# Last 256 features of the last embedding by token, with PSUM banks of their own; query, key and value weight pieces at other places in their tiles

## The chip, the cores and the metric

The kernel runs on one core of one Trainium2 chip. The metric is device microseconds of one execution; the median of several runs counts. A profile is one execution taken by the hardware profiler: TensorE (PE, its weight loads as PEld), VectorE (DVE), ScalarE (ACT), GpSimd (POOL) and the queue that issues DMAs (SP).

## The reference

Two layers over 256 tokens of 1024 features, in float32:

```python
for i in range(DEPTH):                                   # 2 layers
    h = x + 0.5 * swiglu(rms_norm(x, norm_ffn1[i]), w_ffn1_in[i], w_ffn1_out[i])
    u = rms_norm(h, norm_mix[i])
    q, k, v, c, g = jnp.split(u @ w_in[i], splits, axis=-1)
    q = rms_norm(q by head, q_norm[i]); k = rms_norm(k by head, k_norm[i])
    y_attn = window_attention(q, k, v, sink[i], rel_bias) @ w_attn_out[i]
    c_val, c_gate = jnp.split(c, 2, axis=-1)
    c = depthwise_conv(c_val * jax.nn.sigmoid(c_gate), conv_w[i], conv_b[i])   # 31 taps
    y_conv = jax.nn.silu(layer_norm(c, ...)) @ w_conv_out[i]
    g_attn, g_conv = jnp.split(jax.nn.sigmoid(g), 2, axis=-1)
    h = h + (g_attn * y_attn + g_conv * y_conv) @ w_o[i]
    h = h + 0.5 * swiglu(rms_norm(h, norm_ffn2[i]), w_ffn2_in[i], w_ffn2_out[i])
    x = h + (p[i] @ w_pe_proj[i]) * jax.nn.sigmoid(rms_norm(h, norm_pe[i]) @ w_pe_gate[i])
```

The last line is the embedding that the change touches in layer 2; queries, keys and values come out of `u @ w_in`.

## The kernel before, in words

Activations lie by feature: 128 features on the partitions, 256 tokens along the row, eight such blocks for the 1024 features (`x32`). A product of float32 accuracy is made of three matmuls: weights and activations are each split into a high and a low part, and high x high, high x low and low x high are added up in PSUM (`mm3`, whose matmuls have line 339). As a rule a 128x128 block of weights is loaded into PE and 256 columns of activations move past it. One such product of 1024 features takes 8 blocks x 3 = 24 matmuls. In a profile's row `out<-moving,loaded` the first name behind the arrow is what moves.

`Weights` streams all weights through `raw` tiles by DMA and prepares pieces ahead of their use: ACT writes the high part (`w_hi`, line 108), DVE the low part (`w_lo`, line 109), each into one of 7 tiles of 128x1024 words, 4096 bytes a partition. Where a piece starts in SBUF follows from the tile. Before the change each piece starts at its tile's start, a multiple of 256 bytes. Tiles of activations that move past weights are 2112 words for eight blocks (`rows`, with 64 spare words) and start at word 4 of their tile; with the sizes of all tiles ahead of them that is 48 bytes past a multiple of 64 for all of them, high and low parts 256 bytes apart within 512.

In the mixer keys and values (lines 733 to 735) and queries (777 to 779) are made by token: there the activations of 128 tokens are loaded, and the piece of weights moves, 256 columns for keys and values and 512 for queries. Each makes 48 matmuls in a layer. Behind them ACT, POOL and DVE make head norms (`junk`, `ms`, `rh`, lines 709 to 719). DVE runs the 31 taps of the depthwise convolution for four blocks (`y`, line 669) beside all this; at the mixer's end it normalizes `y` by token (`six`, `mv`, `rs`, `yn`, lines 971 to 978), and PE transposes `yn` back (`ps_yc`, line 991). ACT turns gates by a sigmoid (line 932) in between, and DVE multiplies by them (line 956).

The embedding of a layer (`embed`): `project(i)` makes p @ w_pe_proj for four blocks of features into a PSUM tile `pe[i]`; `one(f)` makes the gate of block f (24 matmuls into `ps_pe`), and its evacuation scales by the norm (DVE, line 1117), takes the sigmoid (ACT, line 1118), multiplies by the projection (DVE, line 1120) and adds to `x32` (DVE, line 1121). In layer 2 `put(f)` then transposes the block to tokens (PE, `ps_out`, line 1132), copies it to an output tile `ot` (ACT, line 1134) that shares two buffers with the product `hh`, and issues a DMA (SP, line 1135).

PSUM tiles of one bank come from a pool of four (`mm_tile`), those of two banks from a pool of two (`at_tile`). The order of instructions on each engine is set by a scheduler when the program is built, except where the code pins it. An evacuation is queued and issued behind the first product of the next group.

Of the kernel before, what the change touches and what calls it, by code (L numbers as in the profile page):

```python
# [15 lines left out]
P = 128  # L16
T = 256
# [15 lines left out]
NEG = -1e9  # L33
LOOK = 6
RAW_BUFS = 5
DMA_SCRATCH = 8192
BACKGROUND = 800
WEIGHTS_LAG = 100
ATTN = 7
# [7 lines left out]
class Weights:  # L47
# [14 lines left out]
        self.units.append((k, n, sources))  # L62
        return len(self.units) - 1

    def spec(self, k, n, pieces):

        self.specs.append((k, n, pieces, False))

    def raw_spec(self, unit, k, c0, n):
        self.specs.append((k, n, [(unit, 0, c0, 0, n)], True))  # L70

    def limit(self):
        held = [p[0] for s in self.specs[self.next_get : self.next_prep] if s[3] for p in s[2]]
# [12 lines left out]
    def prep_upto(self, i):  # L86
        nc = self.nc
        while self.next_prep <= min(i, len(self.specs) - 1):
            k, n, pieces, as_is = self.specs[self.next_prep]
            for u, *_ in pieces:  # L90
                self.load_upto(u + RAW_BUFS - 2)
                if u >= self.next_load:
                    return
            if as_is:
                ((u, k0, s0, _, w),) = pieces
                self.ready[self.next_prep] = self.raw[u][:, k0 : k0 + k, s0 : s0 + w]
                self.next_prep += 1
                continue
            hi = self.w_pool.tile([P, KD * P], F32R, name="w_hi")
            lo = self.w_pool.tile([P, KD * P], F32R, name="w_lo")  # L100
            hv = hi[:, : k * n].rearrange("p (k n) -> p k n", n=n)
            lv = lo[:, : k * n].rearrange("p (k n) -> p k n", n=n)
            step = k // self.parts
            for a, (u, k0, s0, d0, w) in ((a, p) for a in range(0, k, step) for p in pieces):
                at = slice(a, a + step)
                src = self.raw[u][:, k0 + a : k0 + a + step, s0 : s0 + w]
                parts = (
                    nc.scalar.copy(out=hv[:, at, d0 : d0 + w], in_=src),  # L108
                    nc.vector.tensor_tensor(  # L109
                        out=lv[:, at, d0 : d0 + w],  # L110
                        in0=src,
                        in1=hv[:, at, d0 : d0 + w].bitcast(F32),
                        op=ALU.subtract,
                    ),
                )
                if self.pin:
                    for ins in parts:
                        self.pin(ins)
                    self.pin = None
            self.ready[self.next_prep] = (hv, lv)  # L120
            self.next_prep += 1
# [34 lines left out]
def encoder_kernel(ctx: ExitStack, tc: tile.TileContext, a: dict, out: bass.AP):  # L156
# [18 lines left out]
    def mm_tile(name):  # L175
        return mmp.tile([P, 512], F32, name=name, tag="mm")
# [84 lines left out]
    def mix_specs(l):  # L261
        w = a["w_in"][l]
        c0 = QD + 2 * P

        def conv_specs(j, n):
            uv = cols_unit(w, KD, c0 + j * P, n * P)
            ug = cols_unit(w, KD, c0 + CD + j * P, n * P)
            for c in range(n):
                ws.spec(KD, P, [(uv, 0, c * P, 0, P)])
                ws.spec(KD, P, [(ug, 0, c * P, 0, P)])  # L270

        conv_specs(0, 2)
        ukv = cols_unit(w, KD, QD, 256)
        for i in range(2):
            ws.spec(KC, 256, [(ukv, i * KC, 0, 0, 256)])
        for i in range(2):
            uq = cols_unit(w[i * KC * P : (i + 1) * KC * P], KC, 0, QD)
            for k in range(0, KC, 2):
                ws.spec(2, QD, [(uq, k, 0, 0, QD)])
        conv_specs(2, 2)  # L280
        g0 = QD + 2 * P + 2 * CD
        for j in range(8):
            u = cols_unit(w, KD, g0 + j * 256, 256)
            for c in range(2):
                ws.spec(KD, P, [(u, 0, c * P, 0, P)])
        w = a["w_attn_out"][l]
        for j in range(2):
            src = w[:, j * 512 : (j + 1) * 512].rearrange("(v c p) n -> v p c n", v=2, p=HD)
            u = ws.unit(KC, 512, [
                (lambda v: v[0:HD], src[0]),  # L290
                (lambda v: v[HD : 2 * HD], src[1]),
            ])
            for c in range(2):
                ws.raw_spec(u, KC, c * 256, 256)
        w = a["w_conv_out"][l]
        for j in range(2):
            u = cols_unit(w, KC, j * 512, 512)
            for c in range(2):
                ws.spec(KC, 256, [(u, 0, c * 256, 0, 256)])
        w = a["w_o"][l]  # L300
        for j in range(4):
            u = cols_unit(w, KD, j * 256, 256)
            for c in range(2):
                ws.spec(KD, P, [(u, 0, c * P, 0, P)])

    def pe_specs(l):
        up = cols_unit(a["w_pe_proj"][l], 2, 0, 1024)
        for c in range(2):
            ws.spec(2, 512, [(up, 0, c * 512, 0, 512)])
        for j in range(4):  # L310
            u = cols_unit(a["w_pe_gate"][l], KD, j * 256, 256)
            for c in range(2):
                ws.spec(KD, P, [(u, 0, c * P, 0, P)])

    for l in range(L):
        ffn_specs(a["w_ffn1_in"][l], a["w_ffn1_out"][l], quick=l == 0)
# [76 lines left out]
    def flush_urgent():  # L393

        with tc.high_priority(offset=300):
            flush()
# [705 lines left out]
    def embed(l, x_in, st, xn, stat):  # L1102
        pw = [ws.get(), ws.get()]
        pl = late["pT"]
        pe = [None, None]

        def project(i):
            pe[i] = at_tile("ps_pp").rearrange("p (f t) -> p f t", t=T)
            for f in range(4):
                mm3(pe[i][:, f, :], pw[i], pl, cols=slice(f * P, (f + 1) * P))  # L1110

        def one(f):
            ps = mm_tile("ps_pe")

            def evac():
# [5 lines left out]
                nc.vector.tensor_tensor(out=x32[:, f, :], in0=hh, in1=x32[:, f, :], op=ALU.add)  # L1121
                if xn is not None:
                    emit_x(f, pcol("norm_ffn1", l + 1, f), xn, stat)
                elif f < KD - 1:
                    ws.later(2, lambda: put(f))

            group([lambda: mm3(ps[:, :T], ws.get(), x_in)], evac)

        def put(f):
            po = mm_tile("ps_out")  # L1130
            for t in range(2):
                nc.tensor.transpose(po[:, t * P : (t + 1) * P], x32[:, f, t * P : (t + 1) * P], ident)
            ot = tmp.tile([P, 2, P], F32, name="ot", tag="hh")
            nc.scalar.copy(out=ot, in_=po[:, :T].rearrange("p (t q) -> p t q", t=2))
            nc.sync.dma_start(out[0].rearrange("(t p) d -> p t d", p=P)[:, :, f * P : (f + 1) * P], ot)

        project(0)
        for f in range(KD):
            if f == 3:
                project(1)  # L1140
            ws.rest = 1 if f == KD - 1 else 0
            one(f)
        flush_urgent()
        ws.rest, ws.pin = 0, tc.keep_in_program_order
        if xn is None:
            ws.finish()
            put(KD - 1)

    def embed_load(l):
        p_ld = tmp.tile([P, 2, PLE], F32, name="p_ld", tag="gu")  # L1150
# [16 lines left out]
    for l in range(L):  # L1167
# [8 lines left out]
        with tc.tile_pool(name="ffn2_pool", bufs=1) as hp:  # L1176
            xe = tuple(rows(hp, KD, "xe_" + part) for part in "hl")
            stat = Stat()
            ffn(hp, l, x_cur, st, "norm_pe", xe, stat, {0: lambda: embed_load(l), 4: lambda: embed_input(hp)})
            x_cur, st = xe, stat.finish(4)  # L1180
            xn, stat = (new_x("xa", f"xn{l}") if l + 1 < L else None), Stat()
            embed(l, x_cur, st, xn, stat)
            x_cur, st = xn, stat.finish(3)
# [39 lines left out]
```

## Time and profile before

| | |
|---|---|
| median of 3 runs | 1092.87 us (1092.22 to 1093.42) |
| profiled execution | 1092.97 us |
| its span, first to last instruction | 1091.2 us |
| granted TensorE clock | 0.998 of full speed |
| busy: PE, DVE, ACT, POOL | 99%, 75%, 57%, 8% |

The span is what the profile's rows add up to; the 1.77 us by which the execution is longer lie around it. Rows give the start in us from the span's start, the time in us, the engine, the line, and in brackets how long the engine stood idle before and what ended that. Matmuls overlap: a row's time of one matmul is longer than the step from one to the next, so steps are read from starts, or from pieces of the chain with their counts.

### The profile page before, as it was taken

What the parts mean: (1) busy time and instruction counts of PE and PEld (TensorE: products, weight loads), DVE (VectorE), ACT (ScalarE), POOL (GpSimd) and SP (SyncE); (2) the same over time, 40 slices, a digit from 0 to 9 for tenths busy, and PEclk for the clock granted to TensorE, in tenths of its full rate; (3) what the DMA queues carried; (4) which work ended last, traced back from release to release, by engine and by line L of the source; (5) the groups of instructions that cost most, each with busy time, mean ns of one, the idle gap of its engine ahead of it and who ended that gap; (6) DMA issues with size and microseconds to landing.
All of it is one profiled execution on the core that took longest, in us unless ns stands there. A gap on an engine that the chain in (4) does not pass through costs nothing.

```text
span 1091.2 us, 22048 instructions
## 1 busy us (share of the span) xinstructions
PE 1082.8 (99%) x9178; PEld 1061.2 (97%) x9178; DVE 822.0 (75%) x1229; ACT 621.0 (57%) x1040; POOL 84.5 (8%) x123
## 2 busy tenths in 40 slices
PE   9999999999999999999999999999999999999997
PEld 9999999999999999999999999999998999999997
DVE  6876666899989766666886666669999986666664
ACT  7655445676767555445765554557776665554552
POOL 2000001210002000001100000113100100000110
PEclk9999999999999999999999999999999999999999
DMA  9876556556066646546556564566634666564531
GB/s 310 281 250 220 179 166 226 177 170 178 15 230 231 220 166 219 182 167 232 185 177 216 171 210 148 186 229 195 154 117 139 212 200 216 172 207 148 188 115 39
DMA packets 195695, 203.01 MB, mean 186 GB/s; under 512 B 3731, under 2 KB 188899, under 8 KB 195596
## 3 DMA queue, kind: packets, MB, share of 16 engines
q1 hardware_dynamic: 195564, 201.60, 55.9%
q8 instruction: 72, 1.18, 0.4%
q14 instruction: 27, 0.22, 0.1%
q10 hardware_dynamic: 32, 0.01, 0.0%
HBM read 200.53 MB, written 1.06 MB: 185 GB/s over the span
## 4 chain that ended last, share of the span: by engine, by line
PE 92%; DVE 2%; ACT 2%; DMA 1%; issue 1%; POOL 0%; SPq 0%; DVEq 0%; ACTq 0%; POOLq 0%
PE ps_gu L339 41%; PE ps_fo L339 22%; PE ps_g L339 8%; PE ps_c L339 4%; PE ps_pe L339 4%; PE ps_wo L339 4%; PE ps_co L1049 2%; DMA raw<-in_w_ffn_in_dram 1%; DVE w_lo L109 1%; PE ps_pp L339 1%; PE ps_s L818 1%; ACT g L932 1%; PE ps_o L874 1%; PE ps_q L778 1%; PE ps_q L777 1%
## 5 line engine op out<-in xcount | busy, mean ns | idle before, releaser
L109 DVE TENSOR_TENSOR w_lo<-raw,w_hi 128x1024 fp32r<-128x1024 f32 (+2 forms) x377 | 450.9, 1202 | 199.3 <-ACT w_hi L108 199.3
L108 ACT CAST w_hi<-raw 128x1024 fp32r<-128x1024 f32 (+2 forms) x377 | 387.7, 1034 | 365.1 <-PE ps_gu L339 191.0
L339 PE MATMUL ps_fo<-h_hi,w_hi 128*128 128x256 f32 x704 | 193.0, 275 | 0.0
L339 PE MATMUL ps_fo<-h_lo,w_hi 128*128 128x256 f32 x704 | 193.0, 275 | 0.0
L339 PE MATMUL ps_fo<-h_hi,w_lo 128*128 128x256 f32 x704 | 193.0, 275 | 0.0
L339 PEld LDWEIGHTS ps_fo<-h_lo,w_hi 128*128 128x128 f32 x704 | 131.8, 188 | 0.0
L339 PEld LDWEIGHTS ps_fo<-h_hi,w_lo 128*128 128x128 f32 x704 | 131.8, 188 | 0.0
L339 PEld LDWEIGHTS ps_fo<-h_hi,w_hi 128*128 128x128 f32 x704 | 131.8, 188 | 0.0
L443 POOL TENSOR_TENSOR sq_acc<-sq_acc,sq 128x256 f32<-128x256 f32 x56 | 52.6, 939 | 829.2 <-ACT sq L442 828.8
L669 DVE SCALAR_TENSOR_TENSOR y<-cpad,cw,y 128x256 f32<-128x256 f32 x240 | 101.8, 487 | 0.1
L339 PE MATMUL ps_gu<-xf0l,w_hi 128*128 128x256 f32 x352 | 97.0, 276 | 0.0
L339 PE MATMUL ps_gu<-xf1l,w_hi 128*128 128x256 f32 x352 | 97.0, 276 | 0.0
L339 PE MATMUL ps_gu<-xn0h,w_hi 128*128 128x256 f32 x352 | 97.0, 276 | 0.0
L339 PE MATMUL ps_gu<-xf0h,w_hi 128*128 128x256 f32 x352 | 96.9, 275 | 0.0
L339 PE MATMUL ps_gu<-xf1h,w_hi 128*128 128x256 f32 x352 | 96.9, 275 | 0.0
L339 PE MATMUL ps_gu<-xf0h,w_lo 128*128 128x256 f32 x352 | 96.9, 275 | 0.0
L339 PE MATMUL ps_gu<-xf1h,w_lo 128*128 128x256 f32 x352 | 96.9, 275 | 0.0
L339 PE MATMUL ps_gu<-xn0h,w_lo 128*128 128x256 f32 x352 | 96.8, 275 | 0.0
L339 PE MATMUL ps_gu<-xn0l,w_hi 128*128 128x256 f32 x352 | 96.8, 275 | 0.0
L339 PE MATMUL ps_gu<-x0h,w_lo 128*128 128x256 f32 x336 | 92.8, 276 | 0.2 <-DVE w_lo L109 0.2
L339 PE MATMUL ps_gu<-x0h,w_hi 128*128 128x256 f32 x336 | 92.9, 276 | 0.0
L339 PE MATMUL ps_gu<-x0l,w_hi 128*128 128x256 f32 x336 | 92.5, 275 | 0.0
(243 smaller groups left out, 2690.4 us busy)
## 6 DMA issues: line engine op xcount, KB each, us to landing
raw<-in_w_ffn_in_dram SPq DMA_DIRECT2D x86, 1024.0 KB
raw<-in_w_in_dram SPq DMA_DIRECT2D x30, 1024.0 KB
raw<-in_w_ffn_out_dram SPq DMA_DIRECT2D x32, 896.0 KB
raw<-in_w_ffn_out_dram SPq DMA_DIRECT2D x16, 1024.0 KB
raw<-in_w_o_dram SPq DMA_DIRECT2D x8, 1024.0 KB
raw<-in_w_pe_gate_dram SPq DMA_DIRECT2D x8, 1024.0 KB
raw<-in_w_attn_out_dram SPq DMA_DIRECT2D x8, 512.0 KB
raw<-in_w_conv_out_dram SPq DMA_DIRECT2D x4, 1024.0 KB
```

The costliest lines, as they stand in the source:

```text
L108: nc.scalar.copy(out=hv[:, at, d0 : d0 + w], in_=src),
L109: nc.vector.tensor_tensor(out=lv[:, at, d0 : d0 + w], in0=src, in1=hv[:, at, d0 : d0 + w].bitcast(F32), op=ALU.subtract,),
L339: mm = nc.tensor.matmul(ps, wa[:, k0 + k, cols], xa[:, kx, :], start=a, stop=b)
L443: nc.gpsimd.tensor_tensor(out=self.acc, in0=self.acc, in1=sq, op=ALU.add)
L669: last_tap[0] = nc.vector.scalar_tensor_tensor(out=y[:, i, :], in0=src, scalar=w, in1=y[:, i, :], op0=ALU.mult, op1=ALU.add)
L777: nc.tensor.matmul(o_, u[0][:, kx, ts], wh[:, k, :], start=kx == 0, stop=False)
L778: nc.tensor.matmul(o_, u[0][:, kx, ts], wl[:, k, :], start=False, stop=False)
L818: mm = nc.tensor.matmul(ps[v][:, c, :], qT[v * HD : (v + 1) * HD, c, qb * P : (qb + 1) * P], kT[v * HD : (v + 1) * HD, :], start=True, sto ...
L874: mm = nc.tensor.matmul(ps[v * HD : (v + 1) * HD, :], vt[:, b, v * HD : (v + 1) * HD], pT[v][:, b, :], start=b == 0, stop=b == 1,)
L932: tc.keep_in_program_order(nc.scalar.activation(out=gs, in_=gs, func=AF.Sigmoid))
L1049: mm = nc.tensor.matmul(ps[:, c, :], wa[:, k, c * P : (c + 1) * P], ya[:, k, :], start=(i, k) == (0, 0), stop=(i, k) == (2, KC - 1),)
```

## The change

1. In layer 2 the embedding's blocks 6 and 7, the last 256 features, are made by token. Their gate weights come as two pieces of 512 features x 256 columns (`pe_specs`), and `last_two` runs 24 matmuls for each half of the tokens into a PSUM bank of its own, with the weights moving. The projection of these features goes by token as well (`project`). The block's old values are transposed to tokens ahead of the gate, into another bank (`xt`), and the sum of that bank and the product goes straight to an output tile and out by DMA. The norm by token (`r_tok`) is made with the last statistic. Block 5's transposes, copy and DMA stand behind the last matmul (`put(KD - 3, last=True)`).
2. Output tiles of `put` share buffers with `sq` instead of `hh`; those of `last_two` with `gu`.
3. Weight tiles grow by 64 words, 256 bytes; keys' and values' pieces start at word 12 of theirs and queries' at word 32, all others at word 0. The DMA scratch shrinks from 8192 to 4096 bytes. All tiles behind it move by multiples of 256 bytes.

```diff
-DMA_SCRATCH = 8192
+DMA_SCRATCH = 4096
...
-            hi = self.w_pool.tile([P, KD * P], F32R, name="w_hi")
-            lo = self.w_pool.tile([P, KD * P], F32R, name="w_lo")
-            hv = hi[:, : k * n].rearrange("p (k n) -> p k n", n=n)
-            lv = lo[:, : k * n].rearrange("p (k n) -> p k n", n=n)
+            hi = self.w_pool.tile([P, KD * P + ROW], F32R, name="w_hi")
+            lo = self.w_pool.tile([P, KD * P + ROW], F32R, name="w_lo")
+            hv = hi[:, place : place + k * n].rearrange("p (k n) -> p k n", n=n)
+            lv = lo[:, place : place + k * n].rearrange("p (k n) -> p k n", n=n)
...
-            ws.spec(KC, 256, [(ukv, i * KC, 0, 0, 256)])
+            ws.spec(KC, 256, [(ukv, i * KC, 0, 0, 256)], 12)
...
-                ws.spec(2, QD, [(uq, k, 0, 0, QD)])
+                ws.spec(2, QD, [(uq, k, 0, 0, QD)], 32)
...
-                ws.spec(KD, P, [(u, 0, c * P, 0, P)])
+                if l == L - 1 and j == 3:
+                    ws.spec(KC, 256, [(u, c * KC, 0, 0, 256)])
+                else:
+                    ws.spec(KD, P, [(u, 0, c * P, 0, P)])
...
+        def by_token(ps, t, w, x, k0, first, last):
+            ts = slice(t * P, (t + 1) * P)
+            n = w[0].shape[1]
+            for k in range(n):
+                for i, (xa, wa) in enumerate(((x[0], w[0]), (x[0], w[1]), (x[1], w[0]))):
+                    nc.tensor.matmul(
+                        ps, xa[:, k0 + k, ts], wa[:, k, :],
+                        start=first and k == 0 and i == 0, stop=last and k == n - 1 and i == 2,
+                    )
...
-            for f in range(4):
+            whole_ = xn is not None or i == 0
+            for f in range(4 if whole_ else 2):
                 mm3(pe[i][:, f, :], pw[i], pl, cols=slice(f * P, (f + 1) * P))
+            if not whole_:
+                for t in range(2):
+                    by_token(pe[i][:, 2 + t, :], t, [w[:, :, 256:512] for w in pw[i]], pl, 0, True, True)
+
+        def last_two():
+            xt = mm_tile("ps_out").rearrange("p (t n) -> p t n", t=2)
+            for t in range(2):
+                for f in range(2):
+                    nc.tensor.transpose(
+                        xt[:, t, f * P : (f + 1) * P], x32[:, KD - 2 + f, t * P : (t + 1) * P], ident
+                    )
+            ps = [mm_tile("ps_pe")[:, :T] for _ in range(2)]
+            w = [ws.get(), ws.get()]
+            flush()
+            for t in range(2):
+                for i in range(2):
+                    by_token(ps[t], t, w[i], x_in, i * KC, i == 0, i == 1)
+                sg = tmp.tile([P, T], F32, name="sg")
+                nc.scalar.activation(out=sg, in_=ps[t], func=AF.Sigmoid, scale=st.r_tok[:, 2 * t : 2 * t + 1])
+                hh = tmp.tile([P, T], F32, name="hh")
+                nc.vector.tensor_tensor(out=hh, in0=pe[1][:, 2 + t, :], in1=sg, op=ALU.mult)
+                ot = tmp.tile([P, T], F32, name="ot", tag="gu")
+                nc.vector.tensor_tensor(out=ot, in0=xt[:, t, :], in1=hh, op=ALU.add)
+                nc.sync.dma_start(out[0][t * P : (t + 1) * P, D - 2 * P :], ot)
+            put(KD - 3, last=True)
...
-                elif f < KD - 1:
+                elif f < KD - 3:
                     ws.later(2, lambda: put(f))
...
-            ot = tmp.tile([P, 2, P], F32, name="ot", tag="hh")
+            ot = tmp.tile([P, 2, P], F32, name="ot", tag="sq")
...
-        for f in range(KD):
+        for f in range(KD if xn is not None else KD - 2):
...
-            x_cur, st = xe, stat.finish(4)
+            x_cur, st = xe, stat.finish(4, tokens=l == L - 1)
```

PE at the program's end before: three rows of the last gate product (block 7), then the transposes of blocks 5, 6 and 7 (`x32` is turned by `ident`).

```order
L339 MATMUL ps_pe_13372<-xe_h_10855,w_hi_13134 128x256
L339 MATMUL ps_pe_13372<-xe_l_10856,w_hi_13134 128x256
L339 MATMUL ps_pe_13372<-xe_h_10855,w_lo_13135 128x256
L1132 MATMUL ps_out_13415<-ident_92,x32_117 128x128 x2
L1132 MATMUL ps_out_13421<-ident_92,x32_117 128x128 x2
L1132 MATMUL ps_out_13427<-ident_92,x32_117 128x128 x2
```

PE now, from the end of block 5's product (line 342 is the old 339) to the first matmuls by token: transposes of the old values of blocks 6 and 7 (line 1134), of blocks 3 and 4 for output (line 1172), then the first token half (line 1115).

```order
L342 MATMUL ps_pe_13306<-xe_h_10855,w_lo_13070 128x256
L1134 MATMUL ps_out_13343<-ident_92,x32_117 128x128 x4
L1172 MATMUL ps_out_13350<-ident_92,x32_117 128x128 x2
L1172 MATMUL ps_out_13356<-ident_92,x32_117 128x128 x2
L1115 MATMUL ps_pe_13348<-w_hi_13099,xe_h_10855 128x256
L1115 MATMUL ps_pe_13348<-w_lo_13100,xe_h_10855 128x256
L1115 MATMUL ps_pe_13348<-w_hi_13099,xe_l_10856 128x256
```

Ahead of the last 48 matmuls now stand eight transposes in one row, and behind them only the pair of block 5; in the matmuls by token the weights come first behind the arrow, so they move.

DVE's last instructions before, the evacuations of blocks 6 and 7 (scale, product, sum):

```order
L1117 TENSOR_TENSOR sg_13403<-ps_pe_13335,r_x_13132 128x256
L1120 TENSOR_TENSOR hh_13406<-ps_pp_13199,sg_13403 128x256
L1121 TENSOR_TENSOR x32_117<-hh_13406,x32_117 128x256
L1117 TENSOR_TENSOR sg_13409<-ps_pe_13372,r_x_13132 128x256
L1120 TENSOR_TENSOR hh_13412<-ps_pp_13199,sg_13409 128x256
L1121 TENSOR_TENSOR x32_117<-hh_13412,x32_117 128x256
```

DVE's last instructions now, block 5 and the two token halves:

```order
L1157 TENSOR_TENSOR sg_13362<-ps_pe_13306,r_x_13134 128x256
L1160 TENSOR_TENSOR hh_13365<-ps_pp_13207,sg_13362 128x256
L1161 TENSOR_TENSOR x32_117<-hh_13365,x32_117 128x256
L1146 TENSOR_TENSOR hh_13394<-ps_pp_13207,sg_13392 128x256
L1148 TENSOR_TENSOR ot_13396<-ps_out_13343,hh_13394 128x256
L1146 TENSOR_TENSOR hh_13425<-ps_pp_13207,sg_13423 128x256
L1148 TENSOR_TENSOR ot_13427<-ps_out_13343,hh_13425 128x256
```

The scale step is gone from the last two evacuations (ACT's sigmoid scales instead), and the sum goes to an output tile, which needs no transposes and no copy. SP issues that tile's DMA last, one place behind block 5's. Ahead of the last layer's final statistic no engine's order changes.

More of the change, by code (lines that the diff above doesn't have):

```diff
@@ L63, in unit, with spec @@
         return len(self.units) - 1
-    def spec(self, k, n, pieces):
-        self.specs.append((k, n, pieces, False))
+    def spec(self, k, n, pieces, place=0):
+        self.specs.append((k, n, pieces, False, place))
     def raw_spec(self, unit, k, c0, n):
-        self.specs.append((k, n, [(unit, 0, c0, 0, n)], True))
+        self.specs.append((k, n, [(unit, 0, c0, 0, n)], True, 0))
     def limit(self):
@@ L88, in prep_upto @@
         while self.next_prep <= min(i, len(self.specs) - 1):
-            k, n, pieces, as_is = self.specs[self.next_prep]
+            k, n, pieces, as_is, place = self.specs[self.next_prep]
             for u, *_ in pieces:
@@ L1123, in evac, with put @@
                     emit_x(f, pcol("norm_ffn1", l + 1, f), xn, stat)
-                elif f < KD - 1:
+                elif f < KD - 3:
                     ws.later(2, lambda: put(f))
             group([lambda: mm3(ps[:, :T], ws.get(), x_in)], evac)
-        def put(f):
+        def put(f, last=False):
             po = mm_tile("ps_out")
             for t in range(2):
-                nc.tensor.transpose(po[:, t * P : (t + 1) * P], x32[:, f, t * P : (t + 1) * P], ident)
-            ot = tmp.tile([P, 2, P], F32, name="ot", tag="hh")
-            nc.scalar.copy(out=ot, in_=po[:, :T].rearrange("p (t q) -> p t q", t=2))
+                turned = nc.tensor.transpose(po[:, t * P : (t + 1) * P], x32[:, f, t * P : (t + 1) * P], ident)
+                if last:
+                    tc.keep_in_program_order(turned)
+            ot = tmp.tile([P, 2, P], F32, name="ot", tag="sq")
+            copy = nc.scalar.copy(out=ot, in_=po[:, :T].rearrange("p (t q) -> p t q", t=2))
+            if last:
+                tc.keep_in_program_order(copy)
             nc.sync.dma_start(out[0].rearrange("(t p) d -> p t d", p=P)[:, :, f * P : (f + 1) * P], ot)
         project(0)
-        for f in range(KD):
+        for f in range(KD if xn is not None else KD - 2):
             if f == 3:
@@ L1142, in embed @@
             one(f)
+        if xn is None:
+            last_two()
+            ws.finish()
+            return
         flush_urgent()
         ws.rest, ws.pin = 0, tc.keep_in_program_order
[L1145 to L1147 removed]
     def embed_load(l):
```

## The prediction

> **What bounds the kernel now.** I read the page first: the span, the busy shares, and the chain that ended last by engine.
>
> ```profile
> span 1091.2 us, 22048 instructions
> PE 1082.8 (99%) x9178; PEld 1061.2 (97%) x9178; DVE 822.0 (75%) x1229; ACT 621.0 (57%) x1040; POOL 84.5 (8%) x123
> PE 92%; DVE 2%; ACT 2%; DMA 1%; issue 1%; POOL 0%; SPq 0%; DVEq 0%; ACTq 0%; POOLq 0%
> ```
>
> TensorE (PE) is busy all the time and is 92% of the chain. So a change counts only where it shortens the row of matmuls, the end after the last of them, or a place where PE waits. The waits of PE come next; these two are what the change can meet.
>
> ```profile
> PE ps_out L1132 <- DVE x L1121: 1.6, 1, 1.6
> PE ps_yc L991 <- DVE yn L978: 0.5, 2, 0.3
> ```
>
> The first is the end of the program: the last feature's transposes wait for the last evacuation. The second, 0.26 us in each layer, is in the token mixer: there VectorE (DVE), not PE, decides.
>
> **The end.** The chain of waits over the last 32 us, pieces left out:
>
> ```profile
> 1061.19 5.50 PE ps_pe L339 x48
> 1066.69 2.73 PE ps_pp L339 x24
> 1069.42 0.22 PE ps_out L1132 x2
> 1069.64 2.79 PE ps_pe L339 x24
> ...
> 1081.66 2.80 PE ps_pe L339 x24
> ...
> 1084.49 0.44 DVE sg L1117
> 1085.01 0.42 ACT sg L1118
> 1085.45 0.24 DVE hh L1120
> 1085.71 1.85 DMA out_dram<-ot
> 1087.65 0.37 ACT ot L1134
> ```
>
> A group of 24 matmuls costs 2.73 us (113.7 ns each), and 2.79 behind transposes. A pair of transposes costs 0.22. The timeline gives the start of the last matmul and of the evacuation behind it:
>
> ```profile
> 1084.17 0.28 PE L339 MATMUL ps_pe<-xe_h,w_lo 128*128 128x256 f32 x1
> 1085.45 0.42 DVE L1120 TENSOR_TENSOR hh<-ps_pp,sg 128x256 f32<-128x256 f32 x1 [0.54 <-ACT sg L1118]
> 1085.91 0.42 DVE L1121 TENSOR_TENSOR x<-hh,x 128x256 f32<-128x256 f32 x1
> ```
>
> From that matmul's start to the end of the last copy (1087.65 + 0.37 = 1088.02) it is 3.85 us: scale, sigmoid, product, sum, then transposes and a copy that waits for an earlier output DMA to free its buffer. From there to the span's end, 3.18 us of DMA and closing work stay as they are.
>
> **The change at the end, behind the last matmul.** By token no transpose follows: sigmoid on ScalarE (ACT) straight from PSUM, product, sum, DMA. From the rows: matmul start to release 0.32 (1084.17 to 1084.49), sigmoid to product 0.44 (1085.01 to 1085.45), product to sum 0.46, the sum itself 0.42: 1.64. The sigmoid now reads PSUM with a scale by token. The nearest row, a Sqrt from PSUM with a bias operand, takes 0.47 (quoted below) and not 0.42, so 1.69; the bounds are 1.64 and 1.74. Saved: 3.85 - 1.69 = **2.16 us**. Feature 5's transposes (issued last) and their copy do not reach the end: the copy stands behind the second sigmoid and ends about 1.16 after the last matmul's start (0.32 + 0.47 + 0.37), so its DMA issue is past at 1.16 + 0.37 = 1.53, before the sum is done:
>
> ```profile
> L1135 SPq DMA_DIRECT2D out_dram<-ot x8: 372/372/383, 1070.1 to 1088.1; - x8
> ```
>
> Should that issue be late, it costs the last DMA up to 0.37; I take none.
>
> **The change at the end, before the last matmul.** Four terms lengthen PE's row.
> 1. The norm by token adds two small products to the last statistic, four passes on PE. The mixer has the same ones:
>
> ```profile
> 198.53 0.34 PE ps_stat L456 x4
> 201.41 0.47 ACT L408 ACTIVATE sd<-ps_stat,eps 128x256 f32<-128x256 f32 x1
> ```
>
> +0.34. The small ACT and DVE instructions with them delay the first evacuations by a few tenths. The work that hides this is the 48 matmuls of 5.50 us behind the statistic; without that cover it would be about 0.3.
> 2. Half of the second projection goes by token: 12 matmuls, and the gate of the last 256 features 48. In these the weights move and the activations are loaded, as in the mixer's keys and values, queries beside them:
>
> ```profile
> 204.26:210.02 5.76, 5.75 (x48) 5.72 (x48) 0.00 (x0) 1.00 0.72 230
> 210.03:221.22 11.19, 11.19 (x48) 8.80 (x48) 0.00 (x0) 1.00 0.55 185
> ```
>
> Keys and values: 5.76/48 = 120 ns for 256 columns; queries: 233 ns for 512. The other way round it is 113.7. The by-token pieces of the gate stay at place 0, as the keys and values now, so I take 120: 12 x 6.3 ns = +0.08 (bounds 0 and 0.08).
> 3. The rest of the row. Before: five times a pair and a group, 5 x 3.01 = 15.05. After: three of these (9.03), eight transposes (0.88) and 48 matmuls of 120 ns (5.76), 15.67: +0.62 (with 113.7 ns +0.32).
> 4. The wait for feature 5's scale step, which frees the bank of the first token group: its DVE step ends 0.32 + 0.42 = 0.74 us after the last matmul of feature 5 starts; the eight transposes before it last until 0.11 + 0.88 = 0.99. Cost 0; if DVE were a step late, about 0.2. The output buffers that no longer share DVE's product tile take away waits off the path: 0.
>
> Sum of the end: 0.34 + 0.08 + 0.62 - 2.16 = **-1.12 us** (bounds -1.55, with 113.7 ns and 1.64, and -0.4, with the 0.3, 0.2 and 0.37 named above and 1.74).
>
> **The places of query, key and value pieces.** All other moving operands of this kind begin 48 bytes past a multiple of 64; place 12 puts keys and values there too, place 32 leaves queries at a multiple of 64, 128 past one of 256. For keys and values the nearest row is therefore 113.7: 48 x 6.3 ns = 0.30 us for PE in each layer. For queries the ends are 233 ns (nothing) and twice 113.7 (0.27 us a layer); a start of their kind has only their own row, so I take nothing and keep 0.27. A loss is not excluded by any row.
>
> What becomes of 0.30 us? The mixer's rows on DVE, POOL and PE say who waits:
>
> ```profile
> 240.00:260.00 20.00, 20.00 (x168) 18.94 (x168) 20.00 (x49) 14.55 (x32) 2.06 (x6) 1.00 0.55 125
> 211.37 4.38 POOL L715 TENSOR_SCALAR ms<-ms,eps_tok 128x2 f32<-128x2 f32 x2 [15.87 <-DVE y L669]
> 216.02 0.18 DVE L719 RECIPROCAL rh<-rh 128x4 f32<-128x4 f32 x1 [0.43 <-ACT rh L718]
> 294.15 0.69 DVE L956 TENSOR_TENSOR g<-ps_ao,g 128x512 f32<-128x512 f32 x1 [0.25 <-ACT g L932]
> 829.36 0.69 DVE L956 TENSOR_TENSOR g<-ps_ao,g 128x512 f32<-128x512 f32 x1 [0.33 <-ACT g L932]
> 302.19 0.98 PE L991 MATMUL ps_yc<-ident,yn 128*128 128x128 f32 x7 [0.26 <-DVE yn L978]
> ```
>
> The fourth number behind the window is DVE: 20.00 of 20 us. It works through its conv taps without a hole, and PE waits for it at 302.19 already. An earlier PE gains there only what DVE gains. DVE gains at 294.15: it idles 0.25 (0.33 in layer 2) for gates that ACT does once PE's attention output is there, and that shrinks with PE's lead. At 216.02 it could gain up to 0.43, but there the two small POOL instructions of 4.38 us decide, and those run beside DVE's taps, not PE's matmuls; I take none. So a lead of 0.30 gives about 0.25 and 0.30: **-0.55 us** in all. If the lead were not swallowed, and queries gained their 0.27 too, it is 2 x 0.57 = 1.14.
>
> [...]
>
> The rest costs nothing: scratch shrinks by 4096 bytes and each weight tile grows by 256, so tiles move by multiples of 256 bytes. DMAs into raw keep their count and size, and no instruction before the last statistic changes its order.
>
> **Sum.** The profiled execution took 1092.97 us, 0.10 over the median of 1092.87. 1092.97 - 1.12 - 0.55 = **1091.3 us**.
>
> **Rivals.**
> - *The places do nothing*: only the end is left, 1092.97 - 1.12 = 1091.9. For it: no row shows a 256-column by-token piece at any other place. Chance 0.17. [...]
> - *The lead comes through*: DVE moves up too, as POOL's two instructions slip ahead of DVE by the 0.43 at 216.02, and queries gain as well: 1092.97 - 1.12 - 1.14 = 1090.7, and 1090.3 with the lower bound of the end. Against it: DVE's full windows. Chance 0.24.
> - *Slower*: the new stride of weight tiles, 4352 bytes for 4096, sets every second tile 256 bytes off its old phase. If loads from those ran like the by-token pieces, 6.3 ns more, half of PE's 9178 matmuls, nearly all of this kind, would cost up to 29 us: 1120. It decides from (1095.1 - 1091.3)/0.0063 = some 600 matmuls on. Against it: high and low parts of an activation begin 256 bytes apart within 512, so the two operands already meet at both distances, and the rows do not tell them apart:
>
> ```profile
> L339 PE MATMUL ps_fo<-h_hi,w_hi 128*128 128x256 f32 x704 | 193.0, 275 | 0.0
> L339 PE MATMUL ps_fo<-h_lo,w_hi 128*128 128x256 f32 x704 | 193.0, 275 | 0.0
> ```
>
> Chance 0.05.
> - The forecast itself, end shortened and the lead mostly swallowed: 0.54, own range 1090.8 to 1091.9.
>
> **How the numbers follow.** A change of this kernel counts from about 0.2%, 2.19 us: faster is below 1090.7, slower above 1095.1. The rival in which the lead comes through lies at that edge and below it (0.18 of its 0.24), and the forecast's lower edge adds 0.08: faster 0.26. Slower is the stride alone, 0.05. Same is the rest, 0.69. For 8 in 10 the range goes from both lower bounds together, 1092.97 - 1.55 - 1.14 = 1090.3, rounded out to 1090.2, to just over the rival in which places do nothing: 1092.1. What it leaves out is the stride, more to gain than 1.14, and an end as poor as its upper bound.
>
> **What would show it.** Right: the last sum on DVE ends 1.7 us behind the last by-token matmul's start, with no transposes on the chain; four passes of about 0.34 behind the last statistic; 48 by-token matmuls in about 5.76; keys and values 48 in 5.45; the DVE idle at the gates gone, PE's wait at ps_yc still there or longer. Wrong: by-token matmuls of the gate at 113.7, queries well below 11.19, the wait at ps_yc shrunk, or ps_fo and ps_gu groups above 113.7 ns.

## The result and the profile after

The changed kernel takes 1091.22 us (median of 15 runs, 1090.31 to 1092.15); the kernel before took 1093.15 us beside it (15 runs). The ratio is 0.9979, with a 95% interval from 0.9971 to 0.9987. The medians lie 1.93 us, 0.18%, apart; two of the 15 runs of the kernel before took 1095.95 and 1096.85 us. Forecast were 1091.3 us and a range from 1090.2 to 1092.1: the time is inside, 0.1 us from the forecast, and stands at the edge of what counts as a change. The two parts behind it did not both come as forecast. The end gave what was worked out; the mixer gave less than forecast in the profiled execution and twice the forecast in others of the same kernel.

The page after: span, busy shares, and the chain by engine. The execution took 1091.56 us.

```profile
span 1089.8 us, 22045 instructions
PE 1082.7 (99%) x9182; PEld 1061.0 (97%) x9182; DVE 821.0 (75%) x1229; ACT 621.4 (57%) x1039; POOL 86.2 (8%) x123
PE 89%; DVE 5%; ACT 3%; POOL 1%; issue 1%; DMA 1%; SPq 0%; DVEq 0%; POOLq 0%
```

The span is 1.4 us shorter, and PE is busy for the same time. Of the two waits of PE that the prediction showed, the first (ps_out, 1.6 us) is gone from the list; the second stands as it stood:

```profile
PE ps_yc L994 <- DVE yn L981: 0.5, 2, 0.3
```

The chain of waits at the end, pieces left out, answers to the one of before. Line 342 is the old 339, 1115 the matmuls by token, 1134 and 1172 transposes.

```profile
1060.86 0.34 PE ps_stat L459 x4
1061.20 5.59 PE ps_pe L342 x48
1066.79 1.36 PE ps_pp L342 x12
1068.15 1.45 PE ps_pp L1115 x12
...
1078.59 0.44 PE ps_out L1134 x4
1079.02 0.44 PE ps_out L1172 x4
1079.46 5.78 PE ps_pe L1115 x48
1085.24 0.02 issue
1085.26 0.48 ACT sg L1144
1085.74 0.02 issue
1085.77 0.44 DVE hh L1146
```

The last matmul and the last sum in the timeline:

```profile
1084.94 0.28 PE L1115 MATMUL ps_pe<-w_hi,xe_l 128*128 128x256 f32 x1
1086.23 0.42 DVE L1148 TENSOR_TENSOR ot<-ps_out,hh 128x256 f32<-128x256 f32 x1
```

From the start of the last matmul to the end of the last sum it is 1086.23 + 0.42 - 1084.94 = 1.71 us, where 3.85 were. What lies ahead of the last matmul grew by the four passes, the by-token pieces and the eight transposes.

To see where the rest went, I set PE's matmuls of the two traces side by side and counted each from the first key-value matmul of layer 1 (PE starts there at 204.27 before and at 204.13 after; these 0.14 us arise within the first 48 us, by the wait of `ps_rb` for ACT's `cw`, and a wait there is 0.9 us in a repeat of the changed kernel). All numbers are PE's start after minus PE's start before, in us:

```
                                     layer 1   layer 2 (from the start of layer 1)
first query matmul                    -0.32     -0.42
first matmul behind the queries       -0.55     -0.64
transposes of the normed queries      -0.49     -0.59
last probability transposes           -0.19     -0.29
product of the mixer's output (ps_wo) -0.09     -0.19
last instruction                                -1.27
```

So keys and values gave 0.32 and queries 0.23 in each layer, as these two windows show (their length first, then PE and PEld with their instructions of these tiles):

```profile
204.13:209.57 5.44, 5.44 (x48) 5.41 (x48) 0.00 (x0) 1.00 0.78 247
209.57:220.55 10.98, 10.98 (x48) 8.82 (x48) 0.00 (x0) 1.00 0.54 176
```

Of this lead of 0.55 us, 0.10 is left at the mixer's end, in each layer. Most goes at the last probability transposes, where the weight load, that is TensorE, waits for ACT's softmax (another 0.11 us goes at the transposes of the queries):

```profile
283.03 0.86 PEld L865 LDWEIGHTS ps_pt<-ident,s 128*128 128x128 f32 x8 [0.27 <-ACT s L857]
```

The end is worth 1.27 - 0.19 = 1.08 us, the mixers 0.19, the start 0.14: together the 1.41 us of the span.

### The profile page after: what moved, and what is told of

It reads as the page before. It is cut to its first block, busy times and chain, and to the rows that moved or that the text cites. A ratio compares the mean times of both kernels' runs of the same rounds, so it can differ in the third digit from the quotient of the medians.

```text
span 1089.8 us, 22045 instructions
## 1 busy us (share of the span) xinstructions
PE 1082.7 (99%) x9182; PEld 1061.0 (97%) x9182; DVE 821.0 (75%) x1229; ACT 621.4 (57%) x1039; POOL 86.2 (8%) x123
## 4 chain that ended last, share of the span: by engine, by line
PE 89%; DVE 5%; ACT 3%; POOL 1%; issue 1%; DMA 1%; SPq 0%; DVEq 0%; POOLq 0%
PE ps_gu L342 43%; PE ps_fo L342 22%; PE ps_g L342 5%; PE ps_wo L342 4%; PE ps_pe L342 4%; PE ps_c L342 2%; PE ps_co L1052 2%; DVE w_lo L109 2%; DVE y L672 2%; PE ps_ao L949 1%; PE ps_pp L342 1%; ACT w_hi L108 1%; DMA raw<-in_w_ffn_in_dram 1%; ACT s L846 1%; PE ps_pe L1115 1%
```

## Experiments

Where one time is given, the run was made for its trace. "Lead" is always counted as in the table above, from a kernel's own first key-value matmul and against the kernel before.

**The end alone.** All pieces back at place 0.

```diff
-            ws.spec(KC, 256, [(ukv, i * KC, 0, 0, 256)], 12)
+            ws.spec(KC, 256, [(ukv, i * KC, 0, 0, 256)])
...
-                ws.spec(2, QD, [(uq, k, 0, 0, QD)], 32)
+                ws.spec(2, QD, [(uq, k, 0, 0, QD)])
```

> The change with keys', values' and queries' pieces back at word 0 of their (still larger) tiles, so the by-token end is alone. Theory 1 (the end carries the gain, the mixer swallows most of what the places give): the span is 1.1 us below before's and the time 0.2 to 0.3 us above the whole change, with 48 key and value matmuls in 5.76 us and 48 query matmuls in 11.19 us again. Theory 2 (the places carry about half): the time is 1.0 us or more above the whole change.

Measured: 1091.96 us (11 runs) beside 1092.93 before, ratio 0.9991 (0.9982 to 1.0). In its trace the lead is zero within 0.05 us at every point of both mixers, and the end is 1.08 us shorter, to the last 0.01 as in the changed kernel. The end's share is thus shown by itself, and so is that the lead comes from the places. The times do not fit theory 1 as the trace does: this kernel is 0.97 us below the kernel before (medians of runs side by side), the whole change 1.93, so the places add about 0.96 in the timed runs, near theory 2 and well above the 0.19 of the one trace. The intervals, nearly 2 us wide, do not settle it.

**The places alone.** The kernel before, with the larger weight tiles, the smaller scratch and places 12 and 32.

> Before, with only the larger weight tiles, the smaller scratch and the places 12 and 32. Theory 1: PE gains 0.32 us at keys and values and 0.23 at queries in each layer, loses 0.13 of it again at the query transposes (ps_qt) and 0.27 at the probability transposes (ps_pt), and the time is 0.2 to 0.3 us below before. Theory 2: the lead is kept and the time is 1.0 us or more below before. Matmuls of the feed-forward parts stay at 113 to 114 ns either way; the larger stride of the tiles would show there if it cost anything.

Measured: 1091.96 us (11 runs) beside the same 1092.93; the ratio, 0.9997 (0.9988 to 1.0006), leans on two runs of 1095.6 and 1095.9. The median is 0.97 us below, near theory 2, but the interval holds both theories. One of these two is the profiled one. Its loss, 3.2 us, lies ahead of the first mixer. The first half of it is a wait:

```profile
PE ps_rb L585 <- ACT cw L574: 1.6, 1, 1.6
```

The second half follows it: from 50.9 us on, the granted clock (the third number from the end) is 0.5 of full speed for 3.4 us. In the other traces it is 1.0 there.

```profile
50.90:54.30 3.40, 3.40 (x18) 3.40 (x17) 3.40 (x6) 1.57 (x4) 0.00 (x0) 0.50 0.78 249
```
The same wait is 0.9 us in a repeat of the changed kernel, so it comes and goes with the execution; that larger weight tiles have no part in it is not shown.

From the first key-value matmul on, keys and values give 0.32 and queries 0.23 a layer, of which 0.17 and 0.18 are kept; the end is as before, and nothing is lost between the mixers.

**Other places, low and high.** Two kernels in which each piece has a place of its own; the gate by token too.

```diff
-            ws.spec(KC, 256, [(ukv, i * KC, 0, 0, 256)], 12)
+            ws.spec(KC, 256, [(ukv, i * KC, 0, 0, 256)], (4, 8, 16, 28)[2 * l + i])
...
-                ws.spec(2, QD, [(uq, k, 0, 0, QD)], 32)
+                ws.spec(2, QD, [(uq, k, 0, 0, QD)], (0, 4, 8, 12, 16, 20, 24, 28)[4 * l + 2 * i + k // 2])
...
-                    ws.spec(KC, 256, [(u, c * KC, 0, 0, 256)])
+                    ws.spec(KC, 256, [(u, c * KC, 0, 0, 256)], (12, 12)[c])
```

The high one has 20, 32, 44, 60 for keys and values, 32 to 60 in steps of 4 for queries, 44 and 60 for the gate.

> The change with a place of its own for each piece: keys and values at words 4 and 8 (layer 1), 16 and 28 (layer 2), queries at 0, 4, 8, 12 (layer 1) and 16, 20, 24, 28 (layer 2), both gate pieces of the end at 12. Theory M (what counts is where the moving piece begins within 64 bytes; 48 is good): keys and values at 28 and queries at 12 and 28 are as fast as at the best place so far (113.4 and 229 ns or less), the gate pieces take 113.4 instead of 120 ns, all others stay at 120 and 233. Theory R (the distance between the starts of moving and loaded operand counts, within 256 bytes): 12 and 28 differ, and fast places are not 64 bytes apart.

> The same with keys and values at words 20 and 32 (layer 1), 44 and 60 (layer 2), queries at 32, 36, 40, 44 (layer 1) and 48, 52, 56, 60 (layer 2), gate pieces at 44 and 60. Theory M: 44 and 60 are fast everywhere (113.4; queries 229 ns or less), 20 and 32 slow. Theory R: 44 and 60 do not agree with each other and with 12 and 28.

Measured: 1090.77 and 1091.61 us, one run each. The mean step from one matmul's start to the next, by place (in words of 4 bytes):

```
keys, values (256 columns)  0: 120.1   4: 117.1   8: 118.8  12: 113.4  16: 117.9  20: 119.9
                           28: 116.7  32: 117.4  44: 118.5  60: 119.8                         ns
queries (512 columns)       0: 233.4   8: 231.8  24: 226.7  32: 228.8  40: 232.1  56: 226.7  ns
gate by token (256)         0: 120.0  12: 113.5  44: 118.9  60: 118.4 (second half)    ns
```

Of the queries six of 16 places are listed; the other ten lie between 227.8 and 233.6.

My reading that starts 48 bytes past a multiple of 64 give the short steps falls: places 28, 44 and 60 are such starts and take 116.7 to 119.8 ns. Place 12 was the right one for another reason. The gate by token gains at place 12 as keys and values do.

**Half of the taps.** Both kernels here leave out every second tap of the convolution (16 of 31 remain), the first with all pieces at place 0, the second at 12 and 32; otherwise both are the changed kernel. The order of instructions is the same in the two, on every engine.

```diff
-                    for t in range(TAPS):
+                    for t in range(0, TAPS, 2):
```

> The new end alone (query, key and value pieces at place 0) with every second tap of the mixer's convolution left out, so VectorE has 15 x 4 x 0.41 = about 25 us less to do in each layer. It is the partner of the next run; by itself: if VectorE decides the mixer's end, the mixer ends earlier by more than a microsecond in each layer and PE's wait at ps_yc (0.26 us) is gone; if PE decides, the gain is no more than that wait, 0.3 us a layer.

> The same with the pieces at places 12 and 32; the order on every engine is that of the run before. Theory (VectorE's taps swallow PE's lead, at the probability transposes and at ps_yc): with VectorE free the lead of keys and values (0.32 us) and of queries (0.23 us) comes through, so the mixer's last matmul comes 0.5 us earlier in each layer than in the partner, about 1.1 us in both. Rival (the lead is lost for a reason that has nothing to do with the taps): 0.1 us a layer, 0.2 in both, as with all taps.

Measured: 1091.32 and 1089.45 us. Between the two the lead is 0.55 behind the queries and 0.57 at the mixer's end in layer 1, and 1.00 in all at the end of layer 2; the spans' ends differ by 1.01 from the same point. So the lead comes through with fewer taps; how far this is the taps' doing is taken up below, with the table of all layers. That the taps set the time by themselves is not so: without them the first of the two gains only 0.4 us a layer, in which PE's wait at ps_yc goes, and DVE then stands idle for PE:

```profile
290.87 0.69 DVE L904 TENSOR_TENSOR g<-ps_g,r_x 128x512 f32<-128x512 f32 x1 [8.62 <-PE ps_g L342]
```

**A third of the query matmuls left out.** The product of the activations' low part with the weights' high part is not made for the queries.

```diff
                             nc.tensor.matmul(o_, u[0][:, kx, ts], wh[:, k, :], start=kx == 0, stop=False)
-                            nc.tensor.matmul(o_, u[0][:, kx, ts], wl[:, k, :], start=False, stop=False)
-                            nc.tensor.matmul(o_, u[1][:, kx, ts], wh[:, k, :], start=False, stop=kx == KD - 1)
+                            nc.tensor.matmul(o_, u[0][:, kx, ts], wl[:, k, :], start=False, stop=kx == KD - 1)
```

> The changed kernel without the third product of the queries (low part of the activations times high part of the weights): 16 matmuls of 229 ns, 3.7 us of PE, less in each layer. Theory (VectorE decides the mixer's end): the lead turns into waits of PE at the probability transposes and at ps_yc; the mixer ends at most 0.4 us earlier in each layer, the span is 1089.0 to 1089.8. Rival (PE's row decides): 3.7 us a layer, a span of about 1082.5.

Measured: 1093.35 us, above the changed kernel, although PE has 7.3 us less to do. In layer 1 the lead is 4.20 behind the queries, 2.70 at the attention's output, and at ps_yc PE is 0.71 later than before. PE's waits name the places:

```profile
PE ps_yt L970 <- DVE y L672: 4.0, 2, 2.0
PE ps_yc L993 <- DVE yn L980: 2.5, 4, 0.9
PE ps_pt L864 <- ACT s L856: 1.8, 2, 0.9
```

The scheduler puts DVE's taps in another order in this kernel, and the expected 1089.0 to 1089.8 is missed. In this order the taps' last sum (`y`) ends the wait, and a lead of 4.2 us a layer is worth nothing. What it would be worth in the order of the changed kernel this run does not show.

**The last probability transposes later.**

```diff
-                        some(0, 0, KC)
+                        some(0, 0, KD)
                         for v in range(2):
                             attend(1, v)
-                        some(0, KC, KD)
...
-                        some(1, 0, 2)
+                        some(1, 0, KC + 2)
                         gather(1)
-                        some(1, 2, KD)
+                        some(1, KC + 2, KD)
```

> The changed kernel with the last probability transposes, and the product behind them, each 12 matmuls (1.36 us) later in the mixer's row of matmuls. Theory (VectorE decides, the transposes are only the first place where PE meets it): PE's wait of 0.27 us for the softmax is gone, and the same time turns up at ps_yc, whose wait grows from 0.26 to about 0.5 us; the mixer's end moves by less than 0.1 us, the span stays at 1089.8 within 0.2. Rival (the lead was lost only for the early transposes): the wait at ps_yc stays 0.26, the mixer ends 0.25 us earlier in each layer, the span is about 1089.3.

Measured: 1090.72 us, span 1088.9. The wait at ps_yc is 0.26 as ever, and the lead is kept whole: 0.54 and 0.57 us. That is against my theory, that ps_yc would take what ps_pt no longer takes. It fits the rival, but gives more than that expected. The next run, which has the transposes where they were, says why.

**The best places found.** Queries at 24, gate by token at 12.

```diff
-                ws.spec(2, QD, [(uq, k, 0, 0, QD)], 32)
+                ws.spec(2, QD, [(uq, k, 0, 0, QD)], 24)
...
-                    ws.spec(KC, 256, [(u, c * KC, 0, 0, 256)])
+                    ws.spec(KC, 256, [(u, c * KC, 0, 0, 256)], 12)
```

> The changed kernel with the two by-token pieces of the last gate at place 12 and the query pieces at place 24, the best of the two sweeps. The gate's 48 matmuls fall from about 120.4 to 113.5 ns after the first dozen, 0.25 to 0.3 us that nothing covers; queries gain 2 ns each, 0.1 us a layer, which VectorE's row swallows. Expected: 0.3 us below the changed kernel, about 1090.9 us, 0.9977 of the kernel before. If the query gain came through as well: 1090.7.

Measured: 1090.21 us (11 runs) beside 1092.61 before, 2.40 us less; ratio 0.9979 (0.9970 to 0.9988). That is 0.7 us below the 1090.9 expected; each against its own runs of the kernel before, it is 0.5 us better than the changed kernel, where 0.3 was expected. Queries take 10.91 us and the gate by token 5.50:

```profile
209.43:220.34 10.91, 10.91 (x48) 8.82 (x48) 0.00 (x0) 1.00 0.53 171
```

```profile
1078.15 5.50 PE ps_pe L1115 x48
```

The lead, 0.61 a layer, is kept whole (0.69 and 0.67 at ps_wo), with PE's transposes and DVE's taps in the places of the changed kernel. So neither the place of the transposes nor the order decides. The trace shows what does. From the first key-value matmul of layer 1 on, DVE runs within 0.06 us of the kernel before for 33 us, then stands 0.71 us earlier, and 0.65 to 0.71 for the rest of the mixer. At this point it had waited for a cast of ACT; ACT does that cast behind 16 small steps on the normed queries, and these wait for four small instructions on POOL, the Newton step of the query norm (lines 419 to 422, called from `head_norms`). In the changed kernel's profile, POOL, ACT and then DVE at the cast:

```profile
230.68 0.64 POOL L419 TENSOR_TENSOR nwt<-rh 128x16 f32<-128x16 f32 x1 [3.07 <-DVE rh L722]
231.40 1.46 POOL L420 TENSOR_TENSOR nwt<-nwt,ms 128x16 f32<-128x16 f32 x1
232.94 0.29 POOL L421 TENSOR_SCALAR nwt<-nwt 128x16 f32<-128x16 f32 x1
233.32 0.25 POOL L422 TENSOR_TENSOR rh<-rh,nwt 128x16 f32<-128x16 f32 x1
233.61 3.39 ACT L788 ACTIVATE qn<-ps_q,rh 128x64 f32<-128x64 f32 x16 [3.06 <-POOL rh L422]
236.78 1.17 ACT L108 CAST w_hi<-raw 128x1024 fp32r<-128x1024 f32 x1
237.98 1.23 DVE L109 TENSOR_TENSOR w_lo<-raw,w_hi 128x1024 fp32r<-128x1024 f32 x1 [1.11 <-ACT w_hi L108]
```

With the best places, POOL and DVE again:

```profile
230.52 0.30 POOL L419 TENSOR_TENSOR nwt<-rh 128x16 f32<-128x16 f32 x1 [3.07 <-DVE rh L722]
230.89 0.28 POOL L420 TENSOR_TENSOR nwt<-nwt,ms 128x16 f32<-128x16 f32 x1
231.26 0.29 POOL L421 TENSOR_SCALAR nwt<-nwt 128x16 f32<-128x16 f32 x1
231.64 1.06 POOL L422 TENSOR_TENSOR rh<-rh,nwt 128x16 f32<-128x16 f32 x1
237.09 1.23 DVE L109 TENSOR_TENSOR w_lo<-raw,w_hi 128x1024 fp32r<-128x1024 f32 x1 [0.37 <-ACT w_hi L108]
```

The chain ends 29.45 us behind the first key-value matmul in the one and 28.72 behind it in the other, DVE's hole is 1.11 or 0.37. What differs is which POOL instruction is long. With the best places it is the last of the four, in the changed kernel's profile the second, with two more behind it. The section on the forecast looks at the DVE step beside it.

**The activations' start.** PLACE, the word at which all activations begin in their tiles, from 4 to 24.

> The changed kernel with the activations beginning 24 words into their tiles and not 4: 192 bytes past a multiple of 256 and not 112. Theory D (only the distance from the loaded operand's start to the moving one's, modulo 256, sets TensorE's step): the feature-wise matmuls then have a distance of 192, that of the fast keys and values, and keys and values have 112, that of the fast feature-wise ones; both stay at 113.3 to 113.5 ns and the span at 1089.8. Theory A (each operand's own start counts): the moving start of nearly all 9182 matmuls is then one that no row has as fast (keys and values took 117 to 120 ns at every other start tried); at 118 ns the span grows by some 40 us.

Measured: 1094.70 us, span 1092.9. The matmuls of the feed-forward stages keep 113.3 (`ps_fo`) and 114.2 ns (`ps_gu`, 113.9 before) from start to start, keys and values 113 ns in the steady part (mean 114.9 with their first dozen), so theory A with its 40 us falls. But theory D does not hold either: the mixer's output product went from 114.5 ns to 118.4, and queries from 228.8 to 233.1, though for the queries only the loaded operand's start moved. So the step hangs on both starts, and for equal distances not in the same way. The rule is left open.

**The changed kernel profiled twice more**, with nothing changed, to see whether program or execution decides.

> The changed kernel, unchanged, profiled anew. Theory (a race on GpSimd decides): in each layer the four small Newton instructions of the query norm on GpSimd end either 28.7 us behind the first key-value matmul (first of them 0.30 us long) or 29.4 us behind it (first 0.64 us long), from one execution to the next. Where they end at 28.7, VectorE's row comes 0.7 us earlier and PE's lead of 0.55 us is still there at the mixer's last matmul; where they end at 29.4, 0.1 to 0.2 us of it are left. Rival (the program decides: the lead is lost in this kernel because of its order or its addresses): 0.1 us a layer is left in both layers again, whatever GpSimd shows.

> The same once more, for four layers in all: by the theory each layer's lead goes by its own Newton instructions (28.7: 0.55 us kept, 29.4: 0.1 to 0.2); by the rival all keep 0.1.

Measured: 1090.93 and 1091.97 us (the second lost 1.3 us ahead of the first mixer). In all four layers the Newton chain ended at 28.7, and in all four the lead was kept: 0.60, 0.60, 0.55, 0.60 us. POOL's first instruction and the DVE step at the cast, in the first of the two:

```profile
231.01 0.30 POOL L419 TENSOR_TENSOR nwt<-rh 128x16 f32<-128x16 f32 x1 [3.07 <-DVE rh L722]
237.58 1.23 DVE L109 TENSOR_TENSOR w_lo<-raw,w_hi 128x1024 fp32r<-128x1024 f32 x1 [0.37 <-ACT w_hi L108]
```

The rival, that the program decides, is out: the same instructions kept 0.1 us a layer once and 0.55 to 0.60 twice. The table has all layers with full taps and the order of the changed kernel (the late transposes with them). The run with moved activations is left out: other matmuls of its mixers are slower too, and by the transposes of the queries its PE is behind the kernel before.

```
Newton chain ends   layers   lead behind the queries   kept at ps_wo
29.4 us             changed kernel 1, 2                  0.55          0.09, 0.10
                    places alone 1, 2                    0.55, 0.54    0.17, 0.18
                    other places low 1, high 1           0.20, 0.23    0.17, 0.17
28.7 us             changed kernel again, four layers    0.55          0.55 to 0.60
                    transposes later 1, 2                0.55, 0.54    0.54, 0.57
                    best places 1, 2                     0.61, 0.62    0.69, 0.67
                    other places low 2, high 2           0.31, 0.17    0.36, 0.20
                    end alone 1, 2                       0.00          -0.01, 0.00
```

The kernel before has both kinds in one execution: its chain ends at 29.4 in layer 1 and at 28.7 in layer 2, with a hole of DVE of 1.10 and 0.38 us. So the two kinds are older than the change. The last row matters too: with POOL early and no lead of PE nothing is gained, because DVE, 0.70 us earlier at the cast, then waits for PE:

```profile
290.71 0.69 DVE L904 TENSOR_TENSOR g<-ps_g,r_x 128x512 f32<-128x512 f32 x1 [0.30 <-PE ps_g L342]
294.24 0.69 DVE L959 TENSOR_TENSOR g<-ps_ao,g 128x512 f32<-128x512 f32 x1 [0.34 <-ACT g L935]
```

The mixer's end thus follows the later of two rows: PE's, which the places shorten, and DVE's, which POOL's race shifts by 0.7 us. That it is a race was seen and not forced: no kernel here takes it away.

The two kernels with half of the taps belong here too. In layer 1 both have the early kind, which keeps the lead with all taps as well, so that layer says nothing of the taps. In layer 2 the kernel with places 12 and 32 has the late kind (29.4) and still keeps 0.43 of 0.55 us, where all taps leave 0.09 to 0.18. That the late kind loses the lead only beside all taps thus rests on one layer.

## Why the forecast came out as it did

**The end** was right in its steps and its sum: 1.07 to 1.08 us in four traces, forecast 1.12 (bounds 0.4 and 1.55). Behind the last matmul 1.71 us (forecast 1.69); four passes 0.34; eight transposes 0.88; the gate by token 5.78 (5.76); projection pieces by token 1.45 against 1.36, 0.09 for the 0.08 forecast. The wait on the bank's release and block 5's DMA cost nothing, as taken. What was missed is small: from the last statistic's first matmul to the second matmul of the gate behind it, it is 0.56 us before and 1.00 now, 0.44 for the 0.34 of the four passes. The bound of 0.4 was added up wrongly: with the 0.3, 0.2 and 0.37 named there the row grows by 1.91, and 1.91 - 2.11 leaves a gain of 0.20.

**The places, keys and values**: 113.7 ns forecast and 113.4 measured, 0.32 us a layer for 0.30. The reason given (48 past a multiple of 64) was wrong, as the sweep shows; the nearest row was a lucky guide.

**Queries**: "I take nothing and keep 0.27" was the wrong end of the bounds. They gained 0.23 us a layer.

**What becomes of the lead** is the step that failed: 0.55 us forecast for the two mixers, 0.19 in one execution and 1.15 to 1.20 in two others. The prediction read PE's wait of 0.26 us at ps_yc as DVE's taps holding PE, and concluded that an earlier PE gains only what DVE gains. But the wait is 0.25 to 0.27 us in every trace with all taps and all query matmuls, whether PE is there 0.09 or 0.56 us earlier: it moves with PE. In the first repeat:

```profile
301.85 0.98 PE L994 MATMUL ps_yc<-ident,yn 128*128 128x128 f32 x7 [0.26 <-DVE yn L981]
```

With half of the taps it is gone, so DVE's work lies in it, but its start is PE's own transposes and products. And the window of 20.00 busy DVE us began at 240, two microseconds behind a hole in which DVE waited for ACT, and ACT for POOL. In the trace of before:

```profile
238.08 1.22 DVE L109 TENSOR_TENSOR w_lo<-raw,w_hi 128x1024 fp32r<-128x1024 f32 x1 [1.10 <-ACT w_hi L108]
```

Where DVE has a hole, it can move. Where POOL is late, most of the lead is lost, much as the prediction had it, but at the softmax and not at ps_yc. DVE's idle time at the gates, forecast to go, fell to 0.11 us in both layers of the changed kernel's profile. Where POOL is early, that idle time is 0.34 us, as without the lead, and yet the lead comes through.

The rival "the lead comes through" had the right kind of mechanism, POOL's small instructions slipping ahead of DVE's, at the wrong instruction: it named the key norm's at 211.37, and it was the query norm's 20 us later. With 1.07 and 1.15 to 1.20 us it describes two of the three profiled executions of the changed kernel. The forecast's 0.55 us for the mixers lies between the 0.19 of one execution and the 1.15 to 1.20 of the others, and a median over executions of both kinds comes out in between; the timed runs have no traces, so how many were of which kind is not shown. By their medians the end alone and the places alone are each worth 0.97 us, with intervals of nearly 2 us, which puts the mixers nearer to the upper figure. That the time came within 0.1 us is luck. The forecast took off 1.67 us; the runs show 1.93, from a kernel before that took 1093.15 us beside them and not the 1092.97 that the forecast started from.

**The slower rival** is out: with the new stride of weight tiles the large groups of line 342 step as before, 113.3 ns in `ps_fo` and 113.9 in `ps_gu`.

**What stands beside the long POOL instruction** is in both kinds the same DVE step, the low part of a piece of weights, 1.21 to 1.23 us long. In the first profile, L420 (quoted above, 231.40, 1.46 us) starts 0.14 us ahead of that step and ends 0.09 us behind its end:

```profile
231.54 1.23 DVE L109 TENSOR_TENSOR w_lo<-raw,w_hi 128x1024 fp32r<-128x1024 f32 x1
```

In the first repeat L420 starts 0.52 us ahead of the step and takes 0.28. There L422, the last of the four, starts 0.23 us into the step and again ends 0.09 us behind it:

```profile
231.39 0.28 POOL L420 TENSOR_TENSOR nwt<-nwt,ms 128x16 f32<-128x16 f32 x1
231.91 1.21 DVE L109 TENSOR_TENSOR w_lo<-raw,w_hi 128x1024 fp32r<-128x1024 f32 x1
232.14 1.07 POOL L422 TENSOR_TENSOR rh<-rh,nwt 128x16 f32<-128x16 f32 x1
```

So in both kinds one of the four, 1.46 or 1.07 us long, ends 0.09 us behind the same DVE step; the late kind has two more to do afterwards. That it waits for the step is my reading of these ends; no run takes the step away, and none shows by what mechanism the one would hold up the other.

Nor does a run show what makes matmuls of keys and values take 120.1 ns at place 0 and 113.4 at place 12.

## What to carry to other kernels

A wait of the bounding engine is only evidence of another bound if it does not move when that engine comes earlier; follow it back to see whether its chain starts on the same engine. A full window of an engine says nothing of the holes just ahead of it: look there for what moves the whole window, above all small GpSimd instructions beside a busy VectorE, whose time differed here between executions of one program (0.28 or 1.46 us for L420 of the changed kernel), and profile a kernel more than once before putting a microsecond down to the program. Steps of matmuls depended here on where both operands start in their tiles (keys and values 113.4 ns at place 12 and 120.1 at 0; queries 228.8 and, with the loaded operand moved, 233.1), so a sweep of a few places in one kernel is cheap and says more than a rule guessed from one row.

## What the runs showed of the hardware

- From start to start a matmul of 256 columns takes 113.4 to 120.1 ns, one of 512 columns 226.7 to 233.6 ns, by the start of its moving operand (kernel before, changed kernel, the two sweeps). With moved activations, moving the loaded operand's start took the queries from 228.8 to 233.1.
- Behind the pairs of transposes at the end (kernel before and changed kernel), the first step takes 203 to 205 ns and the five to ten after it 115 to 121 each before 113 returns; behind the four passes of the mixer's statistic, after a first step of 205, only one does, with 119. Keys and values at place 0 stay at 120.1 on average.
- One GpSimd instruction on 128x16 (L420) takes 1.46 us in the changed kernel's profile and 0.28 in its first repeat, beside the same VectorE instructions, and 0.7 us of VectorE's row in a mixer hang on which of four is the long one.
- Behind a wait of TensorE of 1.6 us at 48 us, the trace of the places alone shows the granted clock at 0.5 for 3.4 us, from 50.9 us on.
